# One decoder layer: S5 parameter loads moved to GpSimd's queue in parts, and the S5 table work spread over all weight steps of the first feed-forward layer

## The chip, the cores and the metric

The kernel runs on one core of one Trainium2 chip. The metric is the device time of one execution in microseconds (us), the median of several runs. A profile is one execution recorded by the hardware profiler; its times are given from the start of the span, which is the time from the first to the last instruction.

## The reference

The layer works on 256 tokens of width 2048, all in float32. It has three parts, each added to its input: a first feed-forward layer, a mixer, and a second feed-forward layer. The S5 branch of the mixer needs tables that follow from its parameters alone.

```python
def reference(x, ...):
    for l in range(DEPTH):                       # DEPTH = 1
        x = x + 0.5 * swiglu(rms_norm(x, ffn1_norm[l]), ffn1_w1[l], ffn1_w3[l], ffn1_w2[l])
        h = rms_norm(x, mix_norm[l])
        x = x + hybrid_mixer(h, w_in[l], ..., w_out[l])
        x = x + 0.5 * swiglu(rms_norm(x, ffn2_norm[l]), ffn2_w1[l], ffn2_w3[l], ffn2_w2[l])
    return rms_norm(x, final_norm)

def swiglu(x, w1, w3, w2):                       # 2048 -> 5632 -> 2048
    return (jax.nn.silu(x @ w1) * (x @ w3)) @ w2

def s5_branch(u, lam_re, lam_im, log_dt, b_re, b_im, c_re, c_im, ...):
    lam = lax.complex(lam_re, lam_im)            # (64 groups, 64 states)
    lam_bar = jnp.exp(lam * jnp.exp(log_dt)[:, None])
    b_bar = ((lam_bar - 1.0) / lam)[..., None] * lax.complex(b_re, b_im)   # (64, 64, 16)
    bu = einsum('bsgh,gph->bsgp', u, b_bar)
    states = associative_scan(a1 * a2, a2 * x1 + x2)      # over the tokens, a = lam_bar
    y = real(einsum('bsgp,ghp->bsgh', states, lax.complex(c_re, c_im))) + d_skip * u
    ...
```

## The kernel before

**Weights and steps.** Every product streams its weights from memory once, in steps of two 128-row tiles by up to 512 columns, 512 KB a step. `plan` lists all steps in the order of use, and `fetch` (L147 to L157) does the same three things for each: SyncE issues the DMA into `wraw` (four buffers, L152), ScalarE casts it to a high part `whi` (three buffers, L154), and VectorE subtracts to get the low part `wlo` (three buffers, L156). TensorE then runs twelve 512-column matmuls a step (L174): high times high, low times high, high times low, for two row tiles and two token tiles. So ScalarE stands in the path of every step: what holds its queue holds the next `whi`.

**The first feed-forward layer** (`ffn`, L362) has 264 steps: 11 hidden chunks of 16 steps (eight for `w1`, eight for `w3`), six of them first and then four output chunks of `w2` with 12 steps each, then the other five hidden chunks and four output chunks with 10 steps each. The first eight steps are in `start` (L186), which mixes them with the loads and transposes of x and fixes the order of TensorE, ScalarE and VectorE by hand. After the first eight steps of a hidden chunk ScalarE applies SiLU (L384) with the scale `rstd`, which GpSimd computes once (L358) from the sums of squares. VectorE multiplies after the next eight steps (L388), and adds an output chunk to x after its `w2` steps (L404).

**The background tasks.** After each of the other 256 steps `tick` (L107) runs: it adds `rate` to `credit` and emits one task from the list `bg` for each whole credit. In the first feed-forward layer `rate` is 0.5 (L372), one task every second tick. The tasks come from `s5_params` (L502) in this order: eight empty ones; `loads`; eight empty ones; `layout`, which moves lambda and dt to the partitions with three small TensorE operations (L541 to L543); six tasks of VectorE arithmetic (`f_dt`, `f_ea`, `f_ang`, `f_sin`, `f_cos`, `f_fac`) and two of complex products over B; and then for each of eight channel tiles j one task that opens tile j and nine that do it. The nine are `stage_b` and `stage_c` (VectorE), `table` steps 0 to 3 (GpSimd, L690 to L698), `trans` (six transposes on TensorE, then three ScalarE copies into `w1` and `w2`, L724 to L729), `table` steps 4 and 5, `clam` (VectorE, L736 to L741), `kzero` (TensorE and VectorE, L748 to L751), `table` step 6, and `spill`, four GpSimd DMAs of the tile's tables to memory (L757). That makes 106 tasks, which end at tick 212. The mixer emits what is left of the list (`drain_bg`) and later reads the spilled tables back.

**Buffers.** The four tables of a tile come from the pool `s5p` with two buffers each, so tile j can write `w1` and `w2` only when tile j - 2 has been spilled.

**Order.** SyncE's queue keeps the order of the code. On the other engines a scheduler sets each engine's order, except in `start` and for instructions marked with `keep_in_program_order`, which stay behind all that was emitted before them on their engine. The DMAs of `loads` are issued by ScalarE and are marked so (`pin`, L519). An engine runs its queue strictly in order. Tasks set when an instruction is emitted, and the scheduler may place one of an engine with little to do well ahead of that.

Of the kernel before, what the change touches and what calls it, by code (L numbers as in the profile page):

```python
# [16 lines left out]
P = 128  # L17
S = 256                 # tokens
TT = S // P             # token tiles
D = 2048  # L20
DFF = 5632
KD = D // P             # k-tiles of the model width
NC = 512                # columns of one weight chunk
KK = 2                  # k-tiles of one weight step
FCH = DFF // NC         # chunks of the hidden width
HALVES = (6, 5)         # hidden chunks held on chip at a time
H = 4                   # mLSTM heads
DV = 256
L = 64                  # mLSTM chunk
NCK = S // L  # L30
QK0, V0, O0, U0 = 0, 1024, 2048, 3080
OGW = 344               # 1032 columns of o and the gates, in three chunks
NPAIR = 32              # pairs of S5 groups
NJ = 8                  # 128-channel tiles of the S5 width
HC = S // 2             # steps of the decimated S5 scan
EPS = 1e-6
S5_RATE = 0.62
AHEAD = 2
WARM = 7
MAGIC = 12582912.0      # 1.5 * 2**23, rounds to the nearest integer  # L40
LOG2E = 1.4426950408889634
# [18 lines left out]
class _Layer:  # L60
# [8 lines left out]

    # ---------------------------------------------------------------- helpers  # L70
    def pool(self, name, bufs=1, space=None, ctx=None):
# [32 lines left out]
    def plan(self):  # L104
        """Every step's weights, in the order of use: (array, row tile, row tiles, column, columns)."""
        steps = []

        def add(name, ks, c0, n=NC):
            steps.extend((name, k, KK, c0, n) for k in ks[::KK])

        def ffn(l):
            c0 = 0
            for n in HALVES:
                for c in range(c0, c0 + n):
                    add(f"ffn{l}_w1", range(KD), c * NC)
                    add(f"ffn{l}_w3", range(KD), c * NC)
                for o in range(3 if l == 2 and c0 else 4):
                    add(f"ffn{l}_w2", range(4 * c0, 4 * (c0 + n)), o * NC)
                c0 += n
        ffn(1)  # L120
        for c in range(2):
            add("w_in", range(KD), U0 + c * NC)
        for c in range(3):
            add("w_in", range(KD), O0 + c * OGW, OGW)
        for b in (QK0, V0):
            for c in range(2):
                add("w_in", range(KD), b + c * NC)
        for r in (range(4), range(4, 8)):
            for c in range(2):
                add("w_out", r, c * NC)  # L130
        for c in (2, 3):
            add("w_out", range(8), c * NC)
        for c in range(2):
            add("w_glu", range(NJ), c * NC)
        for c in range(4):
            add("w_out", range(8, 16), c * NC)
        ffn(2)
        return steps

# [19 lines left out]
    def step_tok(self, acc, xs, part, w, n, first, last, lo_last=False):  # L159
        """One step's products: hi hi, hi lo and lo hi; lo_last where the weights' low parts come late."""  # L160
        nc = self.nc
# [16 lines left out]
    def gemm_tok(self, acc, xs, view, ks, c0, n, first=True, last=True):  # L178
        """acc[t][token, n] += xs^T w, the activations stationary; ks: pairs (k of xs, row tile of w)."""
        for i in range(0, len(ks), KK):  # L180
            part = ks[i:i + KK]
            w = self.weights(view, part[0][1], len(part), c0, n)
            self.step_tok(acc, xs, part, w, n, first and i == 0, last and i + KK >= len(ks))
            self.tick()

    def start(self, acc, view, gain):  # L186
        """The first product, with the transposes of x between its steps."""
        W = lambda i: self.weights(view, i * KK, KK, 0, NC)
        M = lambda i, w: self.step_tok(acc, self.xs, [(i * KK, 0), (i * KK + 1, 0)], w, NC, i == 0, i == 7, i == 0)
        T = lambda c, halves=(0, 1): self.transpose_x(c, gain, halves)  # L190
# [19 lines left out]
    def gemm_ch(self, acc, xs, view, nk, c0):  # L210
        """acc[nt // 2][channel, (nt % 2) * S + token] = w^T xs for the four 128-column tiles from c0."""
        nc = self.nc
        for k0 in range(0, nk, KK):
            wh, wl = self.weights(view, k0, KK, c0, NC)
            for kk in range(KK):
                k = k0 + kk
                xh, xl = xs(k)
                sp = k == nk - 1
                for nt in range(4):
                    o = acc[nt // 2][:, (nt % 2) * S:(nt % 2 + 1) * S]  # L220
# [10 lines left out]

    # ------------------------------------------------------------- constants
    def setup(self):
# [68 lines left out]
    def warm(self, n):  # L302
        """Keeps the tensor engine's clock up while the first data are on their way."""
        b = self.bank()
        for i in range(n):
            self.tc.keep_in_program_order(self.nc.tensor.matmul(
                b, lhsT=self.idle[:, :P], rhs=self.idle, start=True, stop=True))

    # ------------------------------------------------------- norm and transpose
    def new_xT(self):  # L310
# [49 lines left out]

    # ------------------------------------------------------------------- FFN
    def ffn(self, l, chunk_done):  # L362
        nc = self.nc
        w1, w3, w2 = (f"ffn{l}_{n}" for n in ("w1", "w3", "w2"))
        with ExitStack() as ctx:
# [4 lines left out]
            for hi_, n in enumerate(HALVES):  # L370
                gs = []
                self.rate = 0.5 if l == 1 else 1  # L372
                for c in range(n):
# [35 lines left out]
    def tail(self, w2, gs, c0):  # L409
        """The last 512 columns: the last 256 of them for one token tile after the other."""  # L410
        nc = self.nc
# [88 lines left out]

    # ---------------------------------------------------------- S5 parameters
    def s5_params(self, ctx):  # L502
# [15 lines left out]

        def pin(**kw):  # L519
            self.tc.keep_in_program_order(nc.scalar.dma_start(**kw))  # L520

        def loads():
            for i, nm in enumerate(("lam_re", "lam_im")):
                pin(out=lamrow[:, i, :], in_=self.a[nm][0].rearrange("(i g) p -> i (g p)", g=2))
            pin(out=ldrow, in_=self.a["log_dt"])
            for i, nm in enumerate(("b_re", "b_im")):
                pin(out=braw[i], in_=self.a[nm][0].rearrange("(i g) p h -> (g p) i h", g=2))
            for i, nm in enumerate(("c_re", "c_im")):
                pin(out=craw[i], in_=self.a[nm][0].rearrange("(j r) h p -> (r h) j p", r=8))
        tasks.extend([lambda: None] * 8)  # L530
        tasks.append(loads)
        tasks.extend([lambda: None] * 8)

# [20 lines left out]
        def exp_parts(x, em1, s1, s2):  # L554
            """exp(x) = (1 + em1) * s1 * s2, the scales powers of two."""
            xc, kf, k1, r, acc = T(), T(), T(), T(), T()
# [203 lines left out]
        for j in range(NJ):  # L760
            tasks.append(lambda j=j: tasks.__setitem__(slice(0, 0), per_j(j)))

    def s5_tiles(self, skip=None):
        return [self.s5p.tile([P, w], F32, name=f"s5{nm}") if i != skip else None for i, (nm, w) in
                enumerate((("rot", 1024), ("w1", 512), ("w2", 512), ("k0", 128)))]

    # ----------------------------------------------------------------- mixer
    def mixer(self, chunk_done):
# [4 lines left out]
        with ExitStack() as ctx:  # L773
# [17 lines left out]

            # ---- u, channels on partitions, tokens as (parity, step)
            uT = [mp.tile([P, 4, 2, HC], F32, name=f"uT{i}", tag=f"uT{i}") for i in range(2)]
            u4 = [mp.tile([P, 8, HC], F32, name=f"u4{i}", tag=f"u4{i}") for i in range(2)]

            def evac_u(hf, acc):
# [6 lines left out]
                for q in range(4):  # L803
                    for ta in range(2):
                        r = (q % 2) * 64 + ta * 32
                        nc.gpsimd.dma_start(out=v4[r:r + 32, :, q // 2, :],
                                            in_=uT[hf][q * 32:(q + 1) * 32, :, ta, :])
            # ---- S5, a 128-channel tile at a time
            yT = mp.tile([P, NJ, S], F32, name="yT")
# [98 lines left out]

            # ---- o and the gates, tokens on partitions
            oth = mp.tile([P, TT, 1024], F32, name="oth")  # L910
# [16 lines left out]

            # ---- q and k, channels on partitions, causal convolution
            qkc = mp.tile([P, 8, S], F32, name="qkc", tag="qkc")
# [30 lines left out]

            # ---- v, tokens on partitions, with a column of ones for the denominators
            vx = []
# [68 lines left out]

            # ---- output projection of the heads
            hx = lambda k: (hmh[k // 4][:, k % 4, :], hml[k // 4][:, k % 4, :])
# [18 lines left out]

            # ---- gated linear unit of the S5 branch
            hsh = [mp.tile([P, 4, S], F32R, name=f"hsh{i}", tag=f"uT{i}") for i in range(2)]
# [27 lines left out]
    def gates(self, mp, gt, Dm, em):  # L1082
        """Decay matrices, transposed: Dm[s, h, t] = exp(log weight of step s in step t), zero where s > t."""
        nc = self.nc
# [71 lines left out]

    # ------------------------------------------------------------------ whole
    def run(self):
# [60 lines left out]
```

## Time and profile before

| | |
|---|---|
| device time, median of 3 runs | 1907.91 us (1904.5 to 1909.24) |
| span of the profiled execution | 1903.9 us (its own device time is not given beside it) |
| TensorE busy | 1848.1 us, 97% of the span |
| VectorE, ScalarE, GpSimd busy | 1079.3, 812.1, 324.5 us |
| mean granted TensorE clock | 0.988 of full speed |
| DMA | 358.26 MB, mean 188 GB/s |

In the profile PE is TensorE's matmuls and PEld its weight loads, DVE is VectorE, ACT is ScalarE, POOL is GpSimd, SP is SyncE; a q behind a name is the engine's sequencer, which issues its DMAs. The number in square brackets at the end of a row is the time that the engine was idle just before, and what ended it. A busy TensorE is not one at its peak: matmul ends are modelled. In the 40 equal slices of the page TensorE is busy at nine tenths or more nearly everywhere; the exceptions are the eighth slice (333 to 381 us, in the first feed-forward layer) and those of the mixer's first half.

### The profile page before, as it was taken

To read this page: it belongs to the slowest core of one execution; us is meant where nothing else is said; L and a number is where in the kernel's file an instruction comes from. 1 tells how busy PE (TensorE), PEld (TensorE's weight loads), DVE (VectorE), ACT (ScalarE), POOL (GpSimd) and SP (SyncE) were. 2 spreads that over 40 slices of the span, in tenths; PEclk is the share of its full clock that TensorE was granted. 3 is DMA by queue.
4 is the path that set the end of the run, shared out by engine and by line. 5 is a ranking of instruction groups with operands and counts; after the bars stand their busy time and mean duration, and the time that the engine had idled before them with its cause. 6 is when DMAs were issued, how large, how long until landed. Compare 5 with 4: busy or idle time off the path is not lost.

```text
span 1903.9 us, 24152 instructions
## 1 busy us (share of the span) xinstructions
PE 1848.1 (97%) x9221; PEld 1544.4 (81%) x9221; DVE 1079.3 (57%) x1335; ACT 812.1 (43%) x970; POOL 324.5 (17%) x510
## 2 busy tenths in 40 slices
PE   9999999799999999988879999999999999999998
PEld 7788888588888888987868888888888888888887
DVE  5459655455555545576887765554454444455454
ACT  6344443334444444433534355444443334444443
POOL 1004999200000000164433200000000000000011
PEclk9999999899999999999989999999999999999999
DMA  7766766566666655777656456666665566666554
GB/s 243 180 199 183 215 211 210 181 192 201 197 194 194 199 180 181 190 163 191 144 146 190 165 181 197 195 191 190 189 188 187 188 188 188 189 189 192 189 187 148
DMA packets 201142, 358.26 MB, mean 188 GB/s; under 512 B 22434, under 2 KB 39490, under 8 KB 200898
## 3 DMA queue, kind: packets, MB, share of 16 engines
q1 hardware_dynamic: 186992, 344.58, 61.4%
q0 software_dynamic: 3488, 10.02, 1.5%
q10 hardware_dynamic: 10546, 2.13, 0.6%
q8 instruction: 72, 1.18, 0.3%
q14 instruction: 44, 0.36, 0.1%
HBM read 344.62 MB, written 11.01 MB: 187 GB/s over the span
## 4 chain that ended last, share of the span: by engine, by line
PE 48%; DVE 5%; DMA 1%; issue 1%; ACT 0%; POOL 0%; ACTq 0%; POOLq 0%; DVEq 0%; SPq 0%
PE accb L174 42%; DVE wlo L156 2%; DVE A L857 1%; DMA wraw<-in_w_in_dram 1%; PE accb L224 1%; PE accb L226 1%; PE accb L225 1%; DVE qkc L939 1%; PE tpb L486 1%; PE accb L476 0%; PE accb L474 0%; PE accb L475 0%; DVE qkc L936 0%; PE tpb L842 0%; ACT whi L154 0%
## 5 line engine op out<-in xcount | busy, mean ns | idle before, releaser
L156 DVE TENSOR_TENSOR wlo<-wraw,whi 128x1024 fp32r<-128x1024 f32 (+1 forms) x630 | 787.7, 1253 | 744.7 <-ACT whi L154 744.1
L154 ACT CAST whi<-wraw 128x1024 fp32r<-128x1024 f32 (+1 forms) x630 | 655.5, 1042 | 954.5 <-PE accb L174 846.0
L174 PE MATMUL accb<-wlo,xh 128*128 128x512 f32 (+1 forms) x1568 | 607.0, 387 | 17.0 <-DVE wlo L156 16.9
L174 PE MATMUL accb<-whi,xh 128*128 128x512 f32 (+1 forms) x1568 | 610.5, 390 | 3.1 <-ACT whi L154 3.0
L174 PE MATMUL accb<-whi,xl 128*128 128x512 f32 (+1 forms) x1568 | 605.8, 387 | 0.0
L174 PEld LDWEIGHTS accb<-wlo,xh 128*128 128x128 f32 x1568 | 296.1, 189 | 77.6 <-DVE wlo L156 21.1
L174 PEld LDWEIGHTS accb<-whi,xh 128*128 128x128 f32 x1568 | 296.5, 189 | 61.3 <-ACT whi L154 4.2
L174 PEld LDWEIGHTS accb<-whi,xl 128*128 128x128 f32 x1568 | 296.2, 189 | 58.0
L174 PE MATMUL accb<-whi,gh 128*128 128x512 f32 x664 | 264.3, 398 | 10.8 <-ACT whi L154 10.8
L174 PE MATMUL accb<-wlo,gh 128*128 128x512 f32 x664 | 263.1, 396 | 1.2 <-DVE wlo L156 1.2
L174 PE MATMUL accb<-whi,gl 128*128 128x512 f32 x664 | 263.0, 396 | 0.0
L174 PEld LDWEIGHTS accb<-whi,gh 128*128 128x128 f32 x664 | 125.1, 188 | 41.2 <-ACT whi L154 11.2
L174 PEld LDWEIGHTS accb<-wlo,gh 128*128 128x128 f32 x664 | 125.1, 188 | 31.5 <-DVE wlo L156 1.7
L174 PEld LDWEIGHTS accb<-whi,gl 128*128 128x128 f32 x664 | 125.0, 188 | 30.4
L1183 POOL TENSOR_TENSOR x<-x,fn 128x512 f32<-128x512 f32 x6 | 8.9, 1494 | 699.6 <-ACT junk L317 699.6
L226 PE MATMUL accb<-xh,wlo 128*128 128x256 f32 x256 | 73.9, 289 | 5.8 <-DVE wlo L156 5.8
L696 POOL TENSOR_TENSOR tr<-s5rot,sp 128x128 f32<-128x128 f32 (+6 forms) x112 | 55.0, 492 | 132.7 <-DVE sp L636 129.2
L224 PE MATMUL accb<-xh,whi 128*128 128x256 f32 x256 | 74.9, 293 | 0.0
L225 PE MATMUL accb<-xl,whi 128*128 128x256 f32 x256 | 73.8, 289 | 0.0
L698 POOL TENSOR_TENSOR s5rot<-tr,tr 128x128 f32<-128x128 f32 (+6 forms) x112 | 61.3, 559 | 3.3
L226 PEld LDWEIGHTS accb<-xh,wlo 128*128 128x128 f32 x256 | 50.4, 197 | 6.4 <-DVE wlo L156 6.4
L697 POOL TENSOR_TENSOR tr<-s5rot,sp 128x128 f32<-128x128 f32 (+6 forms) x112 | 52.7, 471 | 0.5 <-DVE sp L634 0.4
(305 smaller groups left out, 1362.8 us busy)
## 6 DMA issues: line engine op xcount, KB each, us to landing
wraw<-in_ffn_w_dram SPq DMA_DIRECT2D x528, 512.0 KB, 3.7
wraw<-in_w_in_dram SPq DMA_DIRECT2D x48, 512.0 KB, 5.1
wraw<-in_w_out_dram SPq DMA_DIRECT2D x32, 512.0 KB, 3.6
wraw<-in_w_in_dram SPq DMA_DIRECT2D x24, 344.0 KB, 5.7
spillrot<-s5rot POOLq DMA_DIRECT2D x8, 512.0 KB, 5.2
spillw<-s5w POOLq DMA_DIRECT2D x16, 256.0 KB, 3.1
s5rot<-spillrot SPq DMA_DIRECT2D x8, 512.0 KB, 7.9
wraw<-in_w_glu_dram SPq DMA_DIRECT2D x8, 512.0 KB, 3.7
```

The source lines that it names most:

```text
L154: nc.scalar.copy(hi, raw)
L156: nc.vector.tensor_sub(lo, raw, hi.bitcast(F32))
L174: nc.tensor.matmul(acc[t][:, :n], lhsT=x, rhs=wt, start=first and t not in seen, stop=last and t not in left)
L224: nc.tensor.matmul(o, lhsT=wh[:, kk, ns], rhs=xh, start=st, stop=False, **kw)
L225: nc.tensor.matmul(o, lhsT=wh[:, kk, ns], rhs=xl, start=False, stop=False, **kw)
L226: nc.tensor.matmul(o, lhsT=wl[:, kk, ns], rhs=xh, start=False, stop=sp, **kw)
L486: nc.tensor.transpose(b[:, o:o + P], s[t][:, kt * P:(kt + 1) * P], self.ident)
L696: G.tensor_tensor(tr[0][:, :, :k], rv[:, 0, :, 0:k], u0, op=ALU.mult)
L697: G.tensor_tensor(tr[1][:, :, :k], rv[:, 1, :, 0:k], u1, op=ALU.mult)
L698: G.tensor_tensor(rv[:, a, :, k:2 * k], tr[0][:, :, :k], tr[1][:, :, :k], op=op)
L857: V.tensor_tensor_scan(At[a + 1][:, q, :], self.R[:, 4 * j + q:4 * j + q + 1].broadcast_to([P, HC]), At[a][:, q, :], 0.0, op0=ALU.mult, op ...
L939: V.scalar_tensor_tensor(o, src[:, w:w + S], self.col("conv_w", w * 8 + j), o, op0=ALU.mult, op1=ALU.add)
```

## The change

The parameters lambda, dt, B and C (`lam_re`, `lam_im`, `log_dt`, `b_re`, `b_im`, `c_re`, `c_im`, 1.08 MB in all) are loaded by 13 DMAs in place of 7. GpSimd issues them and not ScalarE, each in a task of its own, without the mark that keeps the order. Each of the two B arrays is cut into four parts of 64 KB. The empty tasks go from 8 and 8 to 3 and 2. The list has 107 tasks, and the rate is now computed: tasks over steps, 107 / (264 - 8) = 0.418, in place of 0.5, so that the last task falls on the last tick. The rest of the diff takes out comments and docstrings and does nothing.

```diff
-                self.rate = 0.5 if l == 1 else 1
+                self.rate = self.ffn1_rate if l == 1 else 1
...
-        def pin(**kw):
-            self.tc.keep_in_program_order(nc.scalar.dma_start(**kw))
-
-        def loads():
-            for i, nm in enumerate(("lam_re", "lam_im")):
-                pin(out=lamrow[:, i, :], in_=self.a[nm][0].rearrange("(i g) p -> i (g p)", g=2))
-            pin(out=ldrow, in_=self.a["log_dt"])
-            for i, nm in enumerate(("b_re", "b_im")):
-                pin(out=braw[i], in_=self.a[nm][0].rearrange("(i g) p h -> (g p) i h", g=2))
-            for i, nm in enumerate(("c_re", "c_im")):
-                pin(out=craw[i], in_=self.a[nm][0].rearrange("(j r) h p -> (r h) j p", r=8))
-        tasks.extend([lambda: None] * 8)
-        tasks.append(loads)
-        tasks.extend([lambda: None] * 8)
+        def load(**kw):
+            tasks.append(lambda: nc.gpsimd.dma_start(**kw))
+
+        tasks.extend([lambda: None] * 3)
+        for i, nm in enumerate(("lam_re", "lam_im")):
+            load(out=lamrow[:, i, :], in_=self.a[nm][0].rearrange("(i g) p -> i (g p)", g=2))
+        load(out=ldrow, in_=self.a["log_dt"])
+        for i, nm in enumerate(("b_re", "b_im")):
+            src = self.a[nm][0].rearrange("(i g) p h -> (g p) i h", g=2)
+            for q in range(4):
+                load(out=braw[i][:, 8 * q:8 * q + 8, :], in_=src[:, 8 * q:8 * q + 8, :])
+        for i, nm in enumerate(("c_re", "c_im")):
+            load(out=craw[i], in_=self.a[nm][0].rearrange("(j r) h p -> (r h) j p", r=8))
+        tasks.extend([lambda: None] * 2)
...
         for j in range(NJ):
             tasks.append(lambda j=j: tasks.__setitem__(slice(0, 0), per_j(j)))
 
+        n_tasks, n_steps = len(tasks) + 9 * NJ, 2 * FCH * KD // KK + 4 * FCH * 4 // KK
+        self.ffn1_rate = n_tasks / (n_steps - 8)
```

## Rows read from the trace of the kernel before

**Rows 1.** Page, busy share; waits of PE (engine, line, releaser: us, times, longest).
```profile
PE 1848.1 (97%) x9221; PEld 1544.4 (81%) x9221; DVE 1079.3 (57%) x1335; ACT 812.1 (43%) x970; POOL 324.5 (17%) x510
...
PE accb L174 <- ACT whi L154: 13.8, 2, 10.8
```

**Rows 2.** Timeline of ACT, 83 to 92 us (start us, us, engine, line, operation).
```profile
83.22 5.04 ACTq L520 DMA_DIRECT2D braw<-in_b_im_dram  x1
...
91.34 2.94 ACT L154 CAST whi<-wraw 128x1024 fp32r<-128x1024 f32 x3 [8.96 <-issue]
```

**Rows 3.** Timeline of DVE: ends of hidden chunks, first and second feed-forward layer.
```profile
55.43 1.41 DVE L388 SCALAR_TENSOR_TENSOR s<-accb,rstd,s 128x512 f32<-128x512 f32 x2
104.90 1.40 DVE L388 SCALAR_TENSOR_TENSOR s<-accb,rstd,s 128x512 f32<-128x512 f32 x2
...
1204.35 1.41 DVE L388 SCALAR_TENSOR_TENSOR s<-accb,rstd,s 128x512 f32<-128x512 f32 x2
1248.78 1.41 DVE L388 SCALAR_TENSOR_TENSOR s<-accb,rstd,s 128x512 f32<-128x512 f32 x2
```

**Rows 4.** Timeline of DVE: ends of four output chunks, first feed-forward layer.
```profile
320.47 1.28 DVE L404 SCALAR_TENSOR_TENSOR x<-accb,x 128x512 f32<-128x512 f32 x2
...
369.21 1.28 DVE L404 SCALAR_TENSOR_TENSOR x<-accb,x 128x512 f32<-128x512 f32 x2
...
437.54 1.28 DVE L404 SCALAR_TENSOR_TENSOR x<-accb,x 128x512 f32<-128x512 f32 x2
```

**Rows 5.** Timeline of ACT, 326 to 345 us.
```profile
326.19 1.05 ACT L154 CAST whi<-wraw 128x1024 fp32r<-128x1024 f32 x1 [1.75 <-PE accb L174]
340.73 0.59 ACT L724 COPY s5w<-tpb 128x512 f32<-128x512 f32 x1 [13.48 <-DMA spillw<-s5w]
344.56 0.27 ACT L728 COPY s5w<-tpb 128x128 f32<-128x128 f32 x1 [3.25 <-DMA spillw<-s5w]
```

**Rows 6.** Timeline of POOL: first table, first two spills of w.
```profile
167.05 1.82 POOL L696 TENSOR_TENSOR tr<-s5rot,sp 128x4 f32<-128x4 f32 x2 [129.24 <-DVE sp L636]
...
338.29 0.60 POOL L757 DMA_DIRECT2D spillw<-s5w  x1
...
341.21 0.55 POOL L757 DMA_DIRECT2D spillw<-s5w  x1
```

**Rows 7.** One stretch each: us, busy PE, PEld, DVE, ACT, POOL; PEclk, DMA share, GB/s.
```profile
10.00:15.00 5.00, 5.00 (x26) 4.17 (x25) 2.56 (x3) 2.44 (x6) 0.00 (x0) 1.00 1.02 347
25.00:30.00 5.00, 5.00 (x28) 4.25 (x27) 2.36 (x5) 4.55 (x12) 0.00 (x0) 1.00 0.54 176
85.00:90.00 5.00, 4.44 (x20) 3.35 (x18) 0.00 (x0) 0.00 (x0) 0.00 (x0) 1.00 0.97 170
340.00:345.00 5.00, 0.00 (x0) 0.00 (x0) 0.14 (x1) 1.02 (x4) 4.12 (x8) 0.50 0.64 235
```

**Rows 8.** Tiles vecs and lamrow: first TensorE use (min/median/max ns, first to last start).
```profile
L289 PE MATMUL tpb<-ident,vecs x1: 247/247/247, 50.1 to 50.1; 96*128 96x96 f32 x1
...
L541 PE MATMUL tpb<-ident,lamrow x1: 242/242/242, 138.8 to 138.8; 32*128 32x32 f32 x1
```

**Rows 9.** Timeline of POOL, first 40 us.
```profile
6.58 0.14 POOL L690 MEMSET s5rot<- 128x4 f32 x1
...
37.09 0.72 POOL L358 TENSOR_TENSOR rstd<-ms,mhalf 128x2 f32<-128x2 f32 x1 [30.27 <-DVE ms L356]
```

**Rows 10.** Timeline of ACT, first 14 us: the one wait for a weight load.
```profile
12.91 1.05 ACT L154 CAST whi<-wraw 128x1024 fp32r<-128x1024 f32 x1 [2.56 <-DMA wraw<-in_ffn_w_dram]
```

**Rows 11.** Page: ACT's DMA queue; an issue, KB, us to landing.
```profile
q10 hardware_dynamic: 10546, 2.13, 0.6%
...
gb<-in_b_i_dram POOLq DMA_DIRECT2D x1, 2.0 KB, 6.9
```

**Rows 12.** Tiles vecs and spillk: GpSimd's DMA issues (ns min/median/max, first to last start).
```profile
L282 POOL DMA_DIRECT2D vecs<-in_conv_w_dram x1: 509/509/509, 3.0 to 3.0; - x1
...
L757 POOL DMA_DIRECT2D spillk<-s5k x8: 540/540/540, 341.7 to 642.8; - x8
```

## The prediction

> **What bounds the kernel now.** I read the page first. TensorE is busy for 97% of the span [rows 1], so time can be won only where it stands still or runs slow. The waits of TensorE come next. In the first feed-forward layer nearly all of them are on ScalarE's `whi`: 13.8 us in two waits, one of 10.8 [rows 1]. The timelines around the two show that they have different causes, and the chunk intervals show what each costs in full, clock included.
>
> The first is at 89 us. ScalarE issues the seven parameter loads; one issue alone takes 5.04 us, and no cast runs until 91.34 us, after 8.96 us of idle time [rows 2]. In that stretch the engines' DMA share is 0.97 [rows 7]. The hidden chunk in which this falls takes 104.90 - 55.43 = 49.47 us, one of the second feed-forward layer 1248.78 - 1204.35 = 44.43 us [rows 3]. **The first stall costs 5.0 us.**
>
> The second is at 335 us. ScalarE has reached the copies of S5 tile 2 into `w1` and `w2`. It is free at 326.19 + 1.05 = 327.24 us and stands until 340.73, and again until 344.56, both times for the landing of a spill of `w` [rows 5]: tile 2 needs the buffers of tile 0. Those spills are GpSimd's, and GpSimd issues them only at 338.29 and 341.21 us, because its queue has the table work of all eight tiles ahead of them, which began at 167.05 us [rows 6]. TensorE empties its stock of casts, stops, and the granted clock is 0.50 (1.2 of 2.4 GHz) when it comes back [rows 7]. The output chunk takes 369.21 - 320.47 = 48.74 us; the two after it, with the same kind of S5 work, take (437.54 - 369.21) / 2 = 34.17 us [rows 4]. **The second stall costs 14.6 us.**
>
> **The change part by part.** *Comments:* no instruction, nothing.
>
> *Loads off ScalarE.* The seven issues go, and with them the hold on the casts: 5.0 us gained, since the chunk of the second layer shows what is left without them [rows 3].
>
> *Loads on GpSimd.* The 13 new DMAs carry no order mark and wait for no data. GpSimd ran the first memsets of the S5 tables at 6.58 us [rows 9], although the task that emits them comes at tick 60; so I expect the loads there too, right after its setup DMAs, and not at their ticks (10 to 39). This puts them beside the loads of x and of the first weights, where the DMA share is 1.02; only later, from 25 us, is it 0.54 [rows 7]. Bounds: nothing, if they are served from what is left over, and 11.4 us, 0.6% of 1903.9 us, which is what all of ScalarE's DMAs took of the sixteen engines, these loads being half of their bytes [rows 11]. Which value? After the first microseconds only one cast waits for a weight load, that of the third step at 12.91 us [rows 10]; the steps behind it are bound by TensorE. From 8.1 us, when three small issues of 0.51 us [rows 12] are done, to 12.9 us the loads take between none and half of the engines: 0 to 2.4 us. I take the middle, **1.2 us lost**, and keep 0 and 11.4 as ends.
>
> *What is queued behind them on GpSimd.* `rstd`, needed by the first SiLU, ran at 37.09 us [rows 9]. An issue takes 0.509 us for 32 rows and 0.540 us for 128 [rows 12], 0.32 ns a row more. A B or C part has 1024 pieces (128 partitions by 8 runs): 0.83 us by that slope, or 4.3 us if the 540 ns were all for pieces. Three small and ten large issues from 6.58 us end at 16.4 us, or at 51 us. The first bound hides wholly ahead of `rstd`. By the second, `rstd` is 14 us late; of ScalarE's hold of 8.96 us only 5.0 came through [rows 2, 3], so 3.9 are absorbed and 10 us lost. I take 0, as the slope rests on two measured sizes, and keep 10 for a rival.
>
> *The new pace.* `layout` moves from tick 36 to tick 46 (19th of 107 tasks at 0.418 a tick). Tick 6 was at 50.1 us and tick 36 at 138.8 [rows 8]; without the first stall that is (88.7 - 5.0) / 30 = 2.79 us a tick, so `layout` comes at 50.1 + 40 x 2.79 = 161.7 us. From it to the first table passed 167.05 - 138.8 = 28.3 us [rows 6, 8], all VectorE arithmetic that does not wait for ticks; tables from 190.0 us. I expect GpSimd's order unchanged, all tables ahead of the first spill of `w`: the second spill of `w` 174.2 us later [rows 6], at 364.1, landed 344.56 - 341.21 = 3.35 us on [rows 5, 6], at 367.5 us. ScalarE comes to the copies of tile 2 with the 52nd task, at tick 125 and not 102: 327.24 - 5.0 + 23 x 2.85 (34.17 / 12) = 387.8 us. The spill is 20 us early, so **14.6 us gained**. The cover is these 20 us: the table stretch would have to be 12% longer to bring the stall back. Less is not excluded, more is: there is nothing else to win there. What is late next is no engine's wait but TensorE.
>
> *The end.* The tasks now end at tick 256 instead of 212, so tile 7's copies and spills fall on the last `w2` steps, beside the sums of squares. ScalarE is busy 43% overall [rows 1] and TensorE's work is only moved: nothing, up to 1 us.
>
> **Sum.** -5.0 - 14.6 + 1.2 = -18.4 us, a span of 1903.9 - 18.4 = 1885.5 us. The median stands 4.0 us above the span; kept so, it is 1907.9 - 18.4 = 1889.5 us.
>
> A rule that speaks against the first gain: the Trainium skill, DMA: Bandwidth & Descriptors, section "Issuing engines are not separate DMA queues", says that another issuing engine saves only the sequencer's time to initiate, usually small relative to the DMA itself. By it alone the first gain is about nothing, and the sum 1894.5 us. The trace disagrees: that time was 8.96 us of ScalarE's queue.
>
> **The rivals.**
> (a) The loads stay at their ticks, spread over some 80 us. Then the start pays nothing: 1888.3 us. The memset at 6.58 us speaks against it [rows 9].
> (b) Heavier loads on GpSimd or on the engines: up to 10 us for `rstd`, or most of the 11.4 us at the start: 1895 to 1900 us. The same time comes out if moving an issue gains nothing, which the first gain's rows speak against [rows 2, 3].
> (c) The second stall stays, because the scheduler puts the first spill of `w` still later or the tables take over 20 us more: 1907.9 - 5.0 + 1.2 = 1904.1 us, no measurable change. For it: the order was the cause before [rows 6] and is not written in the code.
> (d) Slower: each large load holds GpSimd's queue until the one before it has landed. A small GpSimd load in the start took 6.9 us to land [rows 11]; ten are 69 us, from 8.1 to 77 us. `rstd` is 40 us late, 36 come through, and the time is 1889.5 + 36 = 1925.5 us. It decides for slower when the queue is held beyond 65 us (28 us late, 24 lost), 5.7 us a load. Against it: GpSimd went on to a memset at 6.58 us [rows 9] while that load, issued before it, was still under way; but it was small.
>
> **How the numbers follow.** Forecast 0.46, (a) 0.15, (b) 0.15, (c) 0.13, (d) 0.11. About 0.3% (5.7 us) is what a measurement of this kernel can tell from no change. Forecast, (a) and (b) are faster: 0.76. (c) is the same: 0.13. (d) is slower: 0.11. The range starts at 1884 us (the lowest run, 1904.5, less both stalls is 1884.9) and must reach (c), as (c) and (d) together are more than 0.2: 1884 to 1905 us.
>
> **What would show it.** ScalarE's timeline near 82 us has casts only, and the chunk there takes about 44.4 us. The GpSimd timeline has the 13 loads between 6.6 and 17 us and `rstd` still near 37 to 39 us. The third step's cast moves from 12.9 to about 14 us. `layout` is near 162 us, tables start near 190, and the first spills of `w` come near 361 to 364 us, ahead of the copies of tile 2 near 388. No TensorE wait over 2 us on `whi` is left in the first layer, and all four output chunks take about 34 us. I am wrong if GpSimd has gaps or long issues among the loads, if `rstd` is past 45 us, or if ScalarE still waits for a spill.

## The result, and the profile after

The changed kernel takes 1884.26 us (median, 1881.33 to 1887.48) against 1908.55 us (1904.5 to 1909.24) of the kernel before in the same comparison, 24.3 us less by the medians. The ratio is 0.988, with an interval of 0.986 to 0.989, which is 23.3 us. The profiled execution has a span of 1881.7 us against 1903.9, 22.2 us less. Lines of the code behind the change are three higher than before (the tables' reader L842 is L845).

The page, with busy times and the two DMA queues that the change touches (packets, MB, share of the sixteen engines); then the two longest waits of TensorE (us in total, times, longest):

```profile
PE 1840.2 (98%) x9221; PEld 1539.7 (82%) x9221; DVE 1082.8 (58%) x1335; ACT 811.5 (43%) x970; POOL 340.3 (18%) x523
...
q0 software_dynamic: 4000, 11.10, 1.8%
...
q10 hardware_dynamic: 144, 1.05, 0.1%
```

```profile
PE accb L174 <- DVE wlo L156: 18.4, 11, 5.1
PE accb L226 <- DVE wlo L156: 6.6, 5, 2.9
```

The wait on `whi`, 13.8 us before [rows 1], is gone from the list. Before, ScalarE's queue q10 had 10546 packets and 0.6% [rows 11]; it keeps 144 and 0.1%. GpSimd's queue q0 carries the parameters now; the page of the kernel before has for it:

```profile
q0 software_dynamic: 3488, 10.02, 1.5%
```

Ends of chunks in the first feed-forward layer on VectorE's timeline: the first two hidden chunks; the first, second and fourth output chunk; the last hidden chunk and the last output chunk; then the first hidden chunk of the second layer:

```profile
55.71 1.41 DVE L388 SCALAR_TENSOR_TENSOR s<-accb,rstd,s 128x512 f32<-128x512 f32 x2
...
100.15 1.40 DVE L388 SCALAR_TENSOR_TENSOR s<-accb,rstd,s 128x512 f32<-128x512 f32 x2
...
314.45 1.28 DVE L404 SCALAR_TENSOR_TENSOR x<-accb,x 128x512 f32<-128x512 f32 x2
...
348.89 1.28 DVE L404 SCALAR_TENSOR_TENSOR x<-accb,x 128x512 f32<-128x512 f32 x2
...
417.21 1.28 DVE L404 SCALAR_TENSOR_TENSOR x<-accb,x 128x512 f32<-128x512 f32 x2
...
642.50 1.40 DVE L388 SCALAR_TENSOR_TENSOR s<-accb,rstd,s 128x512 f32<-128x512 f32 x2
...
759.78 1.28 DVE L404 SCALAR_TENSOR_TENSOR x<-accb,x 128x512 f32<-128x512 f32 x2
...
1182.64 1.40 DVE L388 SCALAR_TENSOR_TENSOR s<-accb,rstd,s 128x512 f32<-128x512 f32 x2
```

The same view of the kernel before, last hidden chunk and end of the first layer:

```profile
663.69 1.40 DVE L388 SCALAR_TENSOR_TENSOR s<-accb,rstd,s 128x512 f32<-128x512 f32 x2
...
779.10 1.28 DVE L404 SCALAR_TENSOR_TENSOR x<-accb,x 128x512 f32<-128x512 f32 x2
```

These rows divide the 22.2 us. The second hidden chunk takes 44.44 us (49.47 before [rows 3]), 5.0 less. The second output chunk takes 34.44 (48.74 before [rows 4]), 14.3 less. The whole first layer ends 19.3 us earlier. The mixer, from there to 1182.64, takes 422.86 us against 1204.35 - 779.10 = 425.25, 2.4 less. What is left behind 1182.64 is 699.06 against 699.55 us, 0.5 less.

That the two chunks add up to the whole of the 19.3 us is in part a coincidence. The last four output chunks take 759.78 - 642.50 = 117.28 us, 1.9 us more than before (779.10 - 663.69 = 115.41). TensorE is busy in all of this time in both kernels and has 42 operations more in it after the change (556 against 514): the table work that the slower pace moved there. The other chunks, which it left, are shorter by about as much.

GpSimd's timeline in the start (the bracket: idle time just before, and what ended it):

```profile
7.70 0.53 POOL L520 DMA_DIRECT2D lamrow<-in_lam_re_dram  x1 [1.10 <-DMA vecs<-in_ffn_norm_dram]
...
10.00 2.70 POOL L520 DMA_DIRECT2D braw<-in_b_re_dram  x3
17.15 0.89 POOL L520 DMA_DIRECT2D braw<-in_b_re_dram  x1 [4.46 <-issue]
...
30.00 0.88 POOL L520 DMA_DIRECT2D craw<-in_c_im_dram  x1 [3.79 <-issue]
...
37.35 0.73 POOL L358 TENSOR_TENSOR rstd<-ms,mhalf 128x2 f32<-128x2 f32 x1 [6.25 <-DVE ms L356]
```

All 13 loads run there, ahead of their ticks. The queue is held until 30.9 us, yet `rstd` waits for VectorE's `ms`, not for the loads. ScalarE's longest wait for weights in that stretch, and the DMA share (last column but one):

```profile
12.92 1.05 ACT L154 CAST whi<-wraw 128x1024 fp32r<-128x1024 f32 x1 [2.86 <-DMA wraw<-in_ffn_w_dram]
```

```profile
20.00:25.00 5.00, 5.00 (x23) 4.08 (x22) 4.82 (x7) 3.20 (x6) 1.43 (x2) 1.00 1.07 304
25.00:30.00 5.00, 5.00 (x28) 4.26 (x26) 2.09 (x5) 4.30 (x11) 1.22 (x2) 1.00 0.95 279
```

The cast is at the same time as before [rows 10]. The DMA engines stay full for 5 us and more longer (0.54 before at 25 us [rows 7]), and TensorE is busy all the while. Then the place of the second stall: first GpSimd, then ScalarE.

```profile
365.15 1.09 POOL L757 DMA_DIRECT2D spillw<-s5w  x2
...
387.69 0.54 POOL L757 DMA_DIRECT2D spillw<-s5w  x1 [19.33 <-ACT s5w L728]
```

```profile
385.87 1.05 ACT L154 CAST whi<-wraw 128x1024 fp32r<-128x1024 f32 x1 [1.75 <-PE accb L174]
386.82 0.58 ACT L724 COPY s5w<-tpb 128x512 f32<-128x512 f32 x1
```

The spills of tile 0 still stand behind all the tables, but the copies of tile 2 now come over 20 us after their issue, and it is GpSimd that waits (19.33 us) for ScalarE.

### The profile page after: what moved, and what is told of

The parts are those of the page before. It is cut to its first block, busy times and chain, and to the rows that moved or that the text cites. A ratio compares the mean times of both kernels' runs of the same rounds, so it can differ in the third digit from the quotient of the medians.

```text
span 1881.7 us, 24161 instructions
## 1 busy us (share of the span) xinstructions
PE 1840.2 (98%) x9221; PEld 1539.7 (82%) x9221; DVE 1082.8 (58%) x1335; ACT 811.5 (43%) x970; POOL 340.3 (18%) x523
## 3 DMA queue, kind: packets, MB, share of 16 engines
q10 hardware_dynamic: 144, 1.05, 0.1%
## 4 chain that ended last, share of the span: by engine, by line
PE 48%; DVE 5%; issue 1%; DMA 1%; ACT 1%; POOL 0%; ACTq 0%; POOLq 0%; DVEq 0%
PE accb L174 42%; DVE wlo L156 2%; DVE A L860 1%; PE accb L226 1%; PE accb L224 1%; PE accb L225 1%; DMA wraw<-in_w_in_dram 1%; DVE qkc L942 1%; PE tpb L486 1%; PE accb L474 0%; PE accb L476 0%; PE accb L475 0%; DVE qkc L939 0%; ACT whi L154 0%; PE tpb L845 0%
## 5 line engine op out<-in xcount | busy, mean ns | idle before, releaser
L696 POOL TENSOR_TENSOR tr<-s5rot,sp 128x128 f32<-128x128 f32 (+6 forms) x112 | 62.1, 555 | 151.9 <-DVE sp L636 148.4
L757 POOL DMA_DIRECT2D spillw<-s5w x16 | 8.6, 541 | 274.6 <-ACT s5w L728 259.7
L697 POOL TENSOR_TENSOR tr<-s5rot,sp 128x128 f32<-128x128 f32 (+6 forms) x112 | 57.8, 517 | 0.0
```

Of the source, the lines that this page charges most:

```text
L696: G.tensor_tensor(tr[0][:, :, :k], rv[:, 0, :, 0:k], u0, op=ALU.mult)
L697: G.tensor_tensor(tr[1][:, :, :k], rv[:, 1, :, 0:k], u1, op=ALU.mult)
```

## Experiments

The theory: the loads' hold on ScalarE (stall 1, 5 us) and the wait of tile 2's copies for a spill that stands behind all tables (stall 2, 14.6 us) are separate causes; the new place of the loads removes the first, the new pace the second.

**The loads alone.** The kernel after, with the old rate:

```diff
-        self.ffn1_rate = n_tasks / (n_steps - 8)
+        self.ffn1_rate = 0.5
```

> The changed kernel with the old pace, 0.5 task a tick: only the loads are moved. Theory (two separate stalls): the hidden chunk at 80 to 105 us takes 44.4 us as in the changed kernel, layout comes at tick 38 (near 140 us), GpSimd's spills of w of tile 0 near 343 us, ScalarE reaches the copies of tile 2 at tick 104 near 327 us and waits there for some 17 us, the output chunk takes about 48.7 us; time 1899 (changed kernel plus 14.6) to 1903.5 (kernel before less 5.0). Rival (moving the loads is the whole gain): 1884, no wait for a spill.

Measured: 1899.19 us, ratio 0.9964 (0.9953 to 0.9975), which is 6.9 us less than the kernel before (1907 us in this comparison). Its second hidden chunk takes 101.70 - 57.27 = 44.43 us, so stall 1 is gone; the output chunk takes 365.77 - 317.49 = 48.28 us, so stall 2 is all there. ScalarE's timeline:

```profile
342.88 0.59 ACT L724 COPY s5w<-tpb 128x512 f32<-128x512 f32 x1 [13.24 <-DMA spillw<-s5w]
345.98 0.27 ACT L728 COPY s5w<-tpb 128x128 f32<-128x128 f32 x1 [2.51 <-DMA spillw<-s5w]
```

**The pace alone.** The kernel before, with 106 tasks over 256 steps:

```diff
-                self.rate = 0.5 if l == 1 else 1
+                self.rate = 106 / 256 if l == 1 else 1
```

> The kernel before with the pace 106/256 in place of 0.5 and nothing else: loads still ScalarE's. Theory: the stall at the loads stays (a chunk of about 49.4 us), the wait for the spill is gone because tile 2 comes at tick 124; time 1889 (changed kernel plus 5.0) to 1894 (kernel before less 14.6). Rival (the pace does nothing, the queue move does all): 1908, with the wait for the spill still there.

Measured: 1888.61 us, ratio 0.9911 (0.9894 to 0.9927), 17.0 us less. Stall 2 is gone: tile 0's spills are issued at 362.31 us and the copies of tile 2 start at 386.79 us without a wait. Stall 1 moved with its tick and stayed (ScalarE's timeline):

```profile
93.80 0.40 ACTq L520 DMA_DIRECT2D braw<-in_b_re_dram  x1
94.24 4.79 ACTq L520 DMA_DIRECT2D braw<-in_b_im_dram  x1
...
102.10 2.94 ACT L154 CAST whi<-wraw 128x1024 fp32r<-128x1024 f32 x3 [8.71 <-PE tpb L486]
```

The chunk around it, 99.82 to 147.37 us, takes 47.55 us, 3.1 over an undisturbed one. So stall 1 costs 1.9 us less there than its 5.0, and that much of the 17.0 us belongs to it. The two parts give 6.9 + 17.0 = 23.9 us apart and 23.3 together (0.9878 of 1908): within their intervals they add.

The two issues of the rows load arrays of the same size, 4096 pieces of 64 B each. The first takes 0.40 us, the second 4.79; in the kernel before they take 0.40 and 5.04 us (the second in [rows 2]). So the hold is not a price that such an issue has by itself; it falls on the issue that stands right behind another of this size. What it waits for, no run shows.

**The order in place of the pace.** If stall 2 is GpSimd's order and not the rate as such, holding the tables back behind earlier spills cures it at the old rate. The kernel before, with the first operation of each table kept in program order:

```diff
-                    G.memset(rv[:, 0, :, 0:1], 1.0)
+                    self.tc.keep_in_program_order(G.memset(rv[:, 0, :, 0:1], 1.0))
```

> The kernel before, pace and loads as they were, with the first memset of each tile's table kept in program order on GpSimd, so that a tile's table comes behind the spill of the tile before. Theory (the second stall is the place of the spills of w in GpSimd's queue, not the pace): the spills of tile 0 come near 235 us, no wait for a spill, the stall at the loads stays; time 1889 to 1894, as with the pace alone. Rival (the task density of the old pace is what stalls): the output chunk stays near 48.7 us and the time at 1908.

Measured: 1893.75 us, ratio 0.9931 (0.9912 to 0.9951), 13.2 us less. GpSimd's and ScalarE's timelines:

```profile
214.67 0.55 POOL L757 DMA_DIRECT2D spillw<-s5w  x1 [13.79 <-ACT s5w L728]
```

```profile
327.82 0.58 ACT L724 COPY s5w<-tpb 128x512 f32<-128x512 f32 x1
```

Tile 0 is spilled at 214.67 us in place of 338.29 [rows 6], and the copies of tile 2 run at 327.82 us, as soon as ScalarE is free, without the 13.48 us of wait [rows 5]; the output chunk takes 355.49 - 320.69 = 34.80 us. Stall 1 stays (9.01 us of hold). The same mark on the kernel after, with the rate at 0.5, so the loads' new place with the order instead of the pace:

```diff
-        self.ffn1_rate = n_tasks / (n_steps - 8)
+        self.ffn1_rate = 0.5
...
-                    G.memset(rv[:, 0, :, 0:1], 1.0)
+                    self.tc.keep_in_program_order(G.memset(rv[:, 0, :, 0:1], 1.0))
```

> The changed kernel at the old pace of 0.5, with each tile's table kept behind the spill of the tile before on GpSimd (the edit of the earlier experiment on the order). Theory (the slow pace is worth only the end of the spill wait): the same as the changed kernel, 1883 to 1886, no wait for a spill. Rival (the slow pace brings more than that): over 1888.

Measured: 1885.0 us, ratio 0.9888 (0.9871 to 0.9904). It ends its first layer at 758.58 us (the kernel after: 759.78). Its interval holds the ratio of the kernel after, 0.9878: within it, the pace is worth only what it does to the wait for the spill, and either cure will do.

**A pace between.** The kernel after, more than half way to the old rate:

```diff
-        self.ffn1_rate = n_tasks / (n_steps - 8)
+        self.ffn1_rate = 0.47
```

> The changed kernel at 0.47 task a tick, between the two paces. Theory (a race between ScalarE, paced by ticks, and GpSimd, which is not): layout comes at tick 41 near 148 us, the second spill of w has landed some 207 us later near 355 us, ScalarE reaches the copies of tile 2 at tick 111 near 347 us and waits some 8 us, of which about 3.5 are absorbed; 4 to 5 us lost, 1888.5 to 1890. Rival (the pace costs in proportion): two thirds of the way from 1884.3 to 1899.2, that is 1893.8, without a wait of that size.

Measured: 1896.15 us, ratio 0.9942 (0.9925 to 0.9959), 11.9 us above the kernel after, more than the theory and the rival gave. GpSimd, ScalarE, and the output chunk's ends:

```profile
353.54 1.08 POOL L757 DMA_DIRECT2D spillw<-s5w  x2
```

```profile
356.88 0.58 ACT L724 COPY s5w<-tpb 128x512 f32<-128x512 f32 x1 [8.50 <-DMA spillw<-s5w]
```

```profile
316.01 1.27 DVE L404 SCALAR_TENSOR_TENSOR x<-accb,x 128x512 f32<-128x512 f32 x2
...
358.71 1.28 DVE L404 SCALAR_TENSOR_TENSOR x<-accb,x 128x512 f32<-128x512 f32 x2
```

ScalarE is ready at 348.4 us and stands 8.5 us. The chunk takes 42.70 us, so 8.3 of the 14.6 us of stall 2 are left: hardly anything of the wait is absorbed, where 3.5 us were expected. The first layer ends 8.4 us later than after (768.17 us). The profiled execution is 3.0 us above the median, 15.7 us longer than that of the kernel after; the other 7.3 us of it are 5.0 in the mixer and 2.3 behind it. The mixers of the two kernels as one stretch each, 0.47 first (us, busy PE, PEld, DVE, ACT, POOL; PEclk, DMA share, GB/s):

```profile
768.17:1195.99 427.82, 398.08 (x2538) 354.05 (x2537) 301.32 (x438) 185.03 (x263) 124.58 (x95) 0.97 0.66 174
```

```profile
759.78:1182.64 422.86, 392.91 (x2538) 348.88 (x2537) 306.83 (x438) 187.52 (x265) 125.98 (x95) 0.98 0.66 176
```

TensorE stands idle for 29.74 us in the one and 29.95 in the other. It is busy 5.2 us longer for the same 2538 operations, at a lower granted clock (0.97 and 0.98, means over stretches at 1.2 and 2.4 GHz). So by these rows the mixer is not slower there by more waiting; why the clock is lower, this run does not show.

The wait is no switch. The margin from the landing of the last spill that ScalarE waits for to ScalarE's readiness is -16.3 us with the loads alone (rate 0.5: ready at 329.6, the last wait ends at 346.0 us), -9.1 us here (the last wait ends at 357.5 us) and about +18 us at 0.418 (spills issued from 365.15 us, the second landed some 3.35 us after its issue [rows 5, 6], copies at 386.82). Straight lines through the first two and the last two put its zero between 0.43 and 0.45 (an estimate). So far the gain is about proportional: 6.3 of 14.6 us for 37% of the way from 0.5 to 0.418.

**The loads later.** Does having the loads in the start cost anything? The kernel after, with the loads marked:

```diff
-            tasks.append(lambda: nc.gpsimd.dma_start(**kw))
+            tasks.append(lambda: self.tc.keep_in_program_order(nc.gpsimd.dma_start(**kw)))
```

> The changed kernel with the 13 loads kept in program order on GpSimd, so that they go out one by one at their ticks between about 60 and 140 us and not at the start. Theory: nothing is lost at the start in either, and GpSimd has nothing else to do at either time: within 1.5 us of the changed kernel (1884.3). If the early loads cost the start something (the 1.2 us of the prediction), it is 1883; rival (the early loads are part of the gain, for instance through the mixer): over 1887.

Measured: 1883.66 us, ratio 0.9884 (0.9869 to 0.9899), the same as the kernel after. GpSimd's timeline:

```profile
36.30 0.72 POOL L358 TENSOR_TENSOR rstd<-ms,mhalf 128x2 f32<-128x2 f32 x1 [29.48 <-DVE ms L356]
37.01 0.57 POOL L520 DMA_DIRECT2D lamrow<-in_lam_re_dram  x1
...
54.00 0.88 POOL L520 DMA_DIRECT2D craw<-in_c_im_dram  x1 [1.52 <-issue]
```

The mark does not put a load at its tick; it only keeps it behind what was emitted before it on GpSimd, so the batch runs right behind `rstd`, 37 to 55 us. The first hidden chunk ends at 54.66 us, 1.05 before that of the kernel after. But this end scatters by itself: it is at 55.71, 57.27, 56.41, 54.45 and 54.94 us in five kernels with the loads at the start (after, old rate, 0.47, with the order, two parts), at 55.43, 55.58 and 55.67 in those with the loads on ScalarE (before, pace alone, order alone). So the cost of the place is within one or two us, and its sign stays open. The same bytes run beside the weight loads here too, at 37 to 55 us, and the second hidden chunk still takes 99.09 - 54.66 = 44.43 us. So it was ScalarE's held queue that made stall 1, and not the traffic of the loads.

**GpSimd held longer.** Rival (d) needs the hold to reach past `rstd`. The kernel after, with each load issued twice to the same tile, so that the second must wait for the first:

```diff
-            tasks.append(lambda: nc.gpsimd.dma_start(**kw))
+            tasks.append(lambda: (nc.gpsimd.dma_start(**kw), nc.gpsimd.dma_start(**kw)))
```

> The changed kernel with each of the 13 loads issued twice in a row into the same tile, so that the second waits on GpSimd until the first has landed. It tests the slower rival of the prediction, a held GpSimd queue ahead of rstd. Theory: 13 waits of some 6.4 us hold the queue from 8 to about 100 us, rstd is some 60 us late and all but 4 us of it come through: 1935 to 1945. Rival (a late rstd is hidden by the work on the first chunks): under 1890.

Measured: 1893.93 us, ratio 0.9931 (0.9911 to 0.9951): slower than the kernel after by 9.7 us, far less than was expected. The scheduler put other loads between most pairs, so that few waits were in series. GpSimd's timeline, ScalarE's first SiLU, the stretch 45 to 50 us, and the end of the first hidden chunk:

```profile
45.81 0.88 POOL L520 DMA_DIRECT2D craw<-in_c_im_dram  x1 [1.29 <-DMA craw<-in_c_im_dram]
...
46.84 0.75 POOL L358 TENSOR_TENSOR rstd<-ms,mhalf 128x2 f32<-128x2 f32 x1
```

```profile
47.63 1.26 ACT L384 ACTIVATE s<-accb,rstd 128x512 f32<-128x512 f32 x2 [9.21 <-POOL rstd L358]
```

```profile
45.00:50.00 5.00, 0.12 (x1) 0.12 (x1) 0.14 (x1) 2.37 (x4) 1.78 (x6) 0.70 0.36 105
```

```profile
63.06 1.40 DVE L388 SCALAR_TENSOR_TENSOR s<-accb,rstd,s 128x512 f32<-128x512 f32 x2
```

`rstd` now runs right behind the last load, with no wait for `ms`: 9.5 us later than after (37.35). The SiLU waits 9.21 us for it, TensorE is busy 0.12 of 5 us, and the chunk ends 7.35 us later; the rest of the 9.7 us is in the mixer (425.71 us). So the chain of rival (d) is real (loads, `rstd`, SiLU, TensorE). Of the delay 2.1 us are absorbed, less than the 3.9 of the prediction, so a hold costs time from about 37 plus 2 us on (an estimate from this run).

**Fewer, larger loads.** The kernel after, with each B array in two parts of 2048 pieces, and four empty tasks more so that pace and `layout` stay:

```diff
-            for q in range(4):
-                load(out=braw[i][:, 8 * q:8 * q + 8, :], in_=src[:, 8 * q:8 * q + 8, :])
+            for q in range(2):
+                load(out=braw[i][:, 16 * q:16 * q + 16, :], in_=src[:, 16 * q:16 * q + 16, :])
...
-        tasks.extend([lambda: None] * 2)
+        tasks.extend([lambda: None] * 6)
```

> The kernel after with each B array in two parts of 2048 pieces in place of four of 1024; four empty tasks more keep the rate and the place of layout. In the kernel after, an issue of 1024 pieces holds GpSimd for 0.88 us, and two of the gaps before the next issue are 3.4 and 4.5 us; the batch ends at 30.9 us, ahead of the last sum of squares at 37. If the issue costs so much a piece, one of 2048 holds GpSimd for 1.75 us, the batch ends near 30 us again, since the pieces are the same, rstd runs at 37.4 us and the first hidden chunk ends at 55.7: the same time as the kernel after, 1883 to 1886 us, and the cutting is only a matter of what an issue can carry. Rival: the parts are needed because larger loads hold the queue or the engines longer (ScalarE was held 5 us by one of 4096 pieces): gaps over 5 us, the batch past 37 us, rstd at 40 to 45 us, the first chunk 2 to 7 us later, 1887 to 1892 us.

Measured: 1883.82 us, ratio 0.9882 (0.9865 to 0.9898), the same as the kernel after. GpSimd's timeline:

```profile
9.97 1.21 POOL L520 DMA_DIRECT2D braw<-in_b_re_dram  x1
17.67 1.17 POOL L520 DMA_DIRECT2D braw<-in_b_re_dram  x1 [6.49 <-issue]
24.33 1.15 POOL L520 DMA_DIRECT2D braw<-in_b_im_dram  x1 [5.49 <-issue]
29.99 1.16 POOL L520 DMA_DIRECT2D braw<-in_b_im_dram  x1 [4.52 <-issue]
31.14 0.88 POOL L520 DMA_DIRECT2D craw<-in_c_re_dram  x1
35.75 0.88 POOL L520 DMA_DIRECT2D craw<-in_c_im_dram  x1 [3.73 <-issue]
...
36.78 0.75 POOL L358 TENSOR_TENSOR rstd<-ms,mhalf 128x2 f32<-128x2 f32 x1
```

The time is as the theory gave, its working is not. An issue of 2048 pieces takes 1.15 to 1.21 us and not 1.75, and the gaps are longer, up to 6.49 us. The second part is issued 7.7 us after the first, whose landing takes 6.8 us (median of that array): each part of B waits until the one before has about landed. That is rival (d)'s hold. The last issue ends at 36.63 us, `rstd` comes with no idle time before it, and nothing is lost only because its own data are ready at about the same time (VectorE's `ms` ends at 36.60 us). In four parts there is room to spare, 6.25 us.

**The two kernels once more.** To see how far the mixer's 2.4 us repeat. The kernel before:

> The kernel before once more. Its mixer, from the end of the first feed-forward layer to the first hidden chunk of the second, took 425.25 us in the first profile, that of the kernel after 422.86 and 424.36 us in two. If the change gains nothing in the mixer, this one falls in the same band, 422.5 to 425.5 us; if it is over 426 us, a gain of about 2.4 us in the mixer from the change is more likely. End of the first layer at 779.1 us again, within 0.5 us.

and the kernel after:

> The changed kernel once more, for the scatter of the mixer. Its profile lost 2.4 us more than the first layer explains, all of it in the mixer (422.9 us against 425.3). Theory (the granted clock in the mixer differs between executions, whatever the kernel): the mixer takes anything from 422.5 to 426 us here. Rival (the change makes the mixer faster): 423 us or less again.

Measured: 1907.23 us for the kernel before, 1884.91 for the one after. The mixer took 425.25 and 425.57 us in the two profiles of before and 422.86 and 424.36 in those of after, so 0.9 to 2.7 us less, 1.8 on the average, between the two expectations. Other kernels do not sort it: 425.2 (loads alone), 424.9 (pace alone), 426.3 and 424.8 (with the order), 423.9 and 423.9 (loads behind `rstd`, two parts), 425.7 (loads twice). The second profile of before also has larger stalls, chunks of 50.07 and 49.03 us, and ends the first layer at 780.42 us, outside what was expected.

The granted clock goes with a part of it. The mixer as one stretch in the second profile of after and in the first of before:

```profile
759.74:1184.10 424.36, 396.04 (x2538) 351.64 (x2537) 307.11 (x439) 187.64 (x265) 125.39 (x95) 0.97 0.66 175
```

```profile
779.10:1204.35 425.25, 395.83 (x2538) 351.45 (x2537) 307.03 (x438) 187.70 (x265) 125.95 (x95) 0.97 0.65 175
```

The first profile of after has a clock of 0.98 and 392.91 us of busy TensorE (shown with the rate of 0.47). The same kernel thus has both values: in the 20 us from 879.8 us its clock is 1.00 in the first profile and 0.83 in the second. So 1.5 of the 2.4 us do not repeat with the change, and go with the clock of the execution. Between the two profiles at 0.97 the mixer of after is 0.9 us shorter; whether that is the change, two profiles do not show. The second profile of before, 425.57 us at 0.98, shows that the clock is not all of it.

## Why the prediction was right

It gave 1889.5 us, in a range of 1884 to 1905, and the gain came by the forecast's mechanism. The result lies only 0.3 us inside the lower end of the range, less than the kernel after scatters (1881.33 to 1887.48), so that it lies inside at all has some luck in it. The gain is 5.2 us larger than forecast. Step by step:

- **Stall 1.** Forecast 5.0 us by the chunk interval; the chunk fell by 5.03 us, and the run with the loads alone gained 6.9 us (4.8 to 9.0). The Trainium skill (DMA: Bandwidth & Descriptors, "Issuing engines are not separate DMA queues") calls the sequencer's time, which alone is saved by another issuing engine, usually small. The trace agrees for the first B array, whose issue took 0.40 us, and not for the second, whose issue held ScalarE's queue for 5.04 us.
- **Stall 2.** Forecast 14.6 us; the chunk fell by 14.3 us and the first layer by 19.3 us in all. The times it was built from came out close: `layout` at 162.2 us (forecast 161.7), first table at 186.53 (190.0), tile 0's spills at 365.15 (361 to 364), copies of tile 2 at 386.82 (387.8). The tables began 3.5 us early but took 178.6 us to the first spill, against 171.2 before (338.29 - 167.05 [rows 6]), so that about 18 of the 20 us of margin are there. The run with the order instead of the pace shows the cause directly.
- **Loads at the start, not at their ticks.** Right; rival (a) fell. The step gave 1.2 us lost; the first chunk's end moved by 0.3 us (55.43 to 55.71), less than it scatters. The step assumed that the weight loads lose to the parameter loads from 8.1 to 12.9 us. In fact the large loads began only at 10.00 us, the cast of the third step did not move at all (12.92 us against a forecast of 14), and the next two waited 0.48 and 1.67 us, through which TensorE stayed busy.
- **GpSimd's queue.** `rstd` was not delayed: right. The working was wrong: an issue took 0.88 to 0.89 us (forecast 0.83), but the batch ended at 30.9 us and not at 16.4. The slope of 0.32 ns a row was good, also for 2048 pieces (1.15 by the slope from the 540 ns row, measured 1.15 to 1.21). What the sum lacked is waits between issues, three of them of 3.4 to 4.5 us. The prediction named gaps among the loads as a sign that it is wrong; they did occur and cost nothing, since 6.25 us were left. So this term came out at nothing by slack, and not by its sum.
- **Rival (d)** was therefore right in kind. Its hold is seen among the loads, where three were let through before one waited; its chain to a slower kernel is seen with the loads doubled. That ten waits in series would have made the kernel slower is not shown. What kept it away is that up to 3072 pieces went out without a wait; cut into two parts the hold left nothing to spare, and still cost nothing. Rival (c), 1904.1 us, describes what the loads alone would have left; that run took 1899.2.
- **The end.** Forecast nothing, up to 1 us, as TensorE's work is only moved. Right for the whole: the last four output chunks grew by 1.9 us, and other chunks shrank by about as much.
- **Size of the sum.** The forecast took 18.4 us from 1907.9. Three terms account for the rest. The start took 0.9 us less than given. 2.9 us came behind the first layer, 2.4 in the mixer and 0.5 at the end, where the step had "nothing"; of the mixer's part, 1.5 us went with the granted clock of that execution. The median of after is 2.6 us above its profile's span and not 4.0: 1.4 us. The device time of one execution is 1.7 to 1.8 us above its own span in every run (1883.44 and 1881.7, 1907.23 and 1905.5), so the 4.0 us were 1.7 plus a profiled execution that was faster than the median. The sum 18.4 + 0.9 + 2.9 + 1.4 = 23.6 is the 1907.9 - 1884.26 seen.

What stays open: whether the change makes the mixer faster at all, why the granted clock differs there between executions and is lower at a rate of 0.47, and what the second large issue on ScalarE waits for. Not tried was a kernel with all large loads strictly one after the other at the start.

## What to carry to other kernels

A stall is best sized by the interval of a repeated chunk against an undisturbed twin, not by the wait that the profile lists: the sizes of 5.0 and 14.6 us read that way came out to within 0.3 us, where the list gave 13.8 us for both. When an engine waits for a buffer, look at what stands ahead of the releasing instruction in its queue; a rate change that puts the waiting work behind it and an order mark that puts the releasing work ahead are worth the same here, and the mark has far more margin (spills issued at 214.67 us for copies at 327.82, against 365.15 and 386.82). Before moving loads to an idle engine, find the first thing that needs that engine, and count the waits among the loads, not only their issue times.

## What the runs showed of the hardware

GpSimd's issue of a DMA is priced by pieces and not by bytes: 1024 pieces of 64 B (64 KB) and 1024 of 256 B (256 KB) both take 0.88 us, 2048 of 64 B take 1.15 to 1.21 us. The landing of these loads took 4.1 to 6.7 us in the kernel after. The Trainium skill (Perfetto Trace Analysis, "DMA Instruction — SWDGE (GPSIMD)") says that the profile's duration of such an instruction ends when its descriptors are made and not when the data have moved; 0.88 us beside 4.1 to 6.7 us agrees with it.

GpSimd's queue seems to let only so many pieces be under way. Three loads of 1024 went out without a gap and the fourth, 7.15 us after the first, waited 4.46 us; with 2048 each, the second already waited 6.49 us, until the first had had its 6.8 us to land. Bytes do not sort it: 2048 pieces with 128 KB and 1024 with 256 KB went out one behind the other (29.99 and 31.14 us), two loads of 128 KB did not. By these two kernels the room is at least 3072 and less than 4096 pieces, an estimate. Loads right behind `rstd`, where B's parts land in 4.8 to 5.1 us and not in 6.2 to 6.5 (medians), show the same pattern with shorter gaps (3.00 and 1.95 us in place of 4.46 and 3.38).

ScalarE's queue was held in a like way. The first issue of 4096 pieces took 0.40 us and the second, right behind it, 4.79 to 5.04 us in the four profiles that have them (before twice, pace alone, order alone).

The same parameters are far fewer packets on GpSimd's queue. ScalarE's queue lost 10546 - 144 = 10402 packets and 0.5% of the engines' time; GpSimd's gained 4000 - 3488 = 512 packets and 0.3%.

The two small loads of lambda waited for the landing of setup loads that have nothing to do with them (1.10 us for `in_ffn_norm`, 0.72 us for `in_conv_w`): each stood behind the GpSimd DMA issued eight before it.
